# Taking the weights of a later phase in two steps, in slots shared with the input rows

## The chip, the cores and the metric

The kernel runs on one core of a Trainium2 chip. A core has five engines with queues of their own: TensorE (matrix products, PE in the profile, with its weight loads as PEld), VectorE (DVE), ScalarE (ACT), GpSimd (POOL) and SyncE (SP), which here issues all DMA transfers. Each engine works through a list of instructions that is fixed beforehand; an instruction that needs something of another engine or of a transfer waits for a semaphore, and what stands behind it on its engine waits with it. The metric is the device time of one execution in microseconds (us); lower is better.

## The reference

One decoder layer over 4096 tokens of width 1024: an RMSNorm, one input projection, two groups of heads on its output, and an output projection with residual and a last norm.

```python
h = _rmsnorm(x, norm_gain[layer])
p = h @ w_in[layer]                               # 1024 -> 4224 columns: 33 blocks of 128
ps = p[..., :SHIFT_WIDTH]                         # blocks 0 to 12
ps = ps + (_token_shift(ps) - ps) * shift_mix[layer]
...                                               # RWKV-7 recurrence on ps -> y_a
z_a = p[..., o0:o0 + c_a]                         # blocks 13 to 16
...                                               # q, k, v, z_b: blocks 17 to 32
y_b = _dilated_attention(_rope_partial(q, pos), _rope_partial(k, pos), v)
...                                               # silu gates on y_a and y_b
x = x + jnp.concatenate([y_a, y_b], axis=-1) @ w_out[layer]
return _rmsnorm(x, final_gain)
```

Weights and inputs are float32. The kernel computes large products in float16 with every operand split into two parts (the rounded value and the rest), so a weight block must first be scaled by a power of two, taken from its largest absolute value, and then split.

## The kernel before

The program has four stages in a row: the front, an RWKV phase into which the fill is woven, attention, and the output projection. The front normalises and transposes x, computes blocks 0 to 12 for all tokens, and prepares the other 20 blocks of `w_in` for the fill, which multiplies them later.

The front goes over tiles of 512 tokens, j = 0 to 7. `load_x(j)` loads four blocks of 128 rows (`xr`, four slots), squares and scales them on ScalarE, and transposes them on TensorE in eight groups of four (`xp`, line 404), each into a PSUM tile with the tag `proj`, which has two slots; ScalarE, VectorE and GpSimd make the sums and parts from it (`ss`, `xa`, `xb`, `xc`). `single(j)` multiplies block 12 (`pf`, line 529), `pair(q, j)` for q = 0 to 5 two blocks each by a seven-product scheme (`ps`, line 537). `shift` mixes neighbouring tokens into `o` (three slots) and stores it to `prs`.

Between the pairs of tiles 2 to 7 stands one task each: eight `out_max` (the largest of `w_out`), 20 `spill` and four `out_weights` (splitting `w_out`, with two loads `wor` and 14 stores `wos`). The order of tasks is a list: `tasks = [(out_max, n) for n in range(8)] + [(spill,)] * 4`, then four times `out_weights` and three spills, then four spills. `load_x(j + 1)` is written behind pair 1 of tile j.

A spill (`spill_weights`, line 314) of block b does all of this in one piece: load 512 KB into `wr` (one slot, shared with the loads of `w_out`); the largest absolute value of each row on VectorE (line 266) into `wsm`; the largest over the rows by two small matmuls into a `proj` tile (`max`, lines 274 and 276) with a VectorE reduction between; the power of two and its reciprocal; the two parts into `wl` (line 293 on ScalarE, line 294 on VectorE; one slot, lent to the second load of `out_weights` too); the store of `wl` to `wz` in DRAM (line 320).

What is written here is not the order in which the engines run. A scheduler in the framework goes through the program with its own cost estimates, gives each tile a slot when one is free, places each engine's instructions one by one, earlier written first where several are ready, and fixes that order. So an instruction can move past others when the tiles or slots around it change.

After tile 7, `first_fill` and `fill_weights` load the first operands of the fill, whose products (`pj`, line 706) begin where the front's end; the RWKV phase begins with small loads, whose tiles lie where the front's tiles lay, and its first matmul is `pu` (line 852).

Of the kernel before, what the change touches and what calls it, by code (L numbers as in the profile page):

```python
# [12 lines left out]
F32 = mybir.dt.float32  # L13
# [9 lines left out]
NKT = 8  # L23
# [10 lines left out]
WTOP = 2.0 ** 14  # L34
# [154 lines left out]
class Layer:  # L189
# [71 lines left out]

    def power(self, sm, *xs):

        V = self.nc.vector
        for i, x in enumerate(xs):
            V.tensor_reduce(sm[:, i:i + 1], x, axis=AX.XY if len(x.shape) > 2 else AX.X, op=ALU.max,
                            apply_absolute_value=True)
        if len(xs) > 1:
            V.tensor_max(sm[:, 0:1], sm[:, 0:1], sm[:, 1:2])

        ps = self.RP.tile([128, 132], F32, tag="proj", name=f"max{self.nsum}")
        self.nsum += 1
        P = self.nc.tensor
        P.matmul(ps[0:1, 0:128], lhsT=sm[:, 0:1], rhs=self.ident, start=True, stop=True)
        V.tensor_reduce(sm[0:1, 1:2], ps[0:1, 0:128], axis=AX.X, op=ALU.max)
        P.matmul(ps[:, 128:129], lhsT=self.ones[0:1, :], rhs=sm[0:1, 1:2], start=True, stop=True)
        V.tensor_scalar(sm[:, 1:2], ps[:, 128:129], 1e-30, None, op0=ALU.max)
        V.tensor_scalar(sm[:, 0:1].bitcast(I32), sm[:, 1:2].bitcast(I32), 0x7F800000, None, op0=ALU.bitwise_and)
        V.reciprocal(sm[:, 2:3], sm[:, 0:1])

    def scale(self, wr, b, top, pool):

        V, n = self.nc.vector, len(wr)
        sm = pool.tile([128, 3], F32, tag="wsm", name=f"wsm{b}", bufs=2)
        self.power(sm, *wr)
        V.tensor_scalar(self.usc[:, b:b + n], sm[:, 0:1].to_broadcast([128, n]), self.g2, 1.0 / (top * XS),
                        op0=ALU.mult, op1=ALU.mult)
        V.tensor_scalar(sm[:, 2:3], sm[:, 2:3], top, None, op0=ALU.mult)
        return sm[:, 2:3]
# [21 lines left out]
            V.tensor_scalar(self.ug[:, z:z + 1], self.usc[:, 21 + z:22 + z], self.uh[:, z:z + 1], 1.0 / QS,  # L311
                            op0=ALU.mult, op1=ALU.mult)

    def spill_weights(self, b, pool):

        wr = pool.tile([128, NKT, 128], F32, tag="wr", name=f"wr{b}", bufs=1)
        w = pool.tile([128, 2, NKT, 128], F16, tag="wl", name=f"wl{b}", bufs=1)
        self.load_weights(wr, b)
        self.parts(w, wr, self.scale([wr], b, WTOP, pool))
        self.nc.sync.dma_start(self.wz[b - 13], w)  # L320
        if b < 17:
            self.gate_scales(b - 13, b)
        elif b > 28:
            self.gate_scales(b - 25, b)
# [27 lines left out]
    def front(self):  # L352
# [5 lines left out]
        V, G, S, P = nc.vector, nc.gpsimd, nc.scalar, nc.tensor  # L358
# [3 lines left out]
        sp = ctx.enter_context(tc.tile_pool(name="sF", bufs=2))  # L362
# [71 lines left out]
        def first_fill():  # L434
            self.nx = 0
            self.fx = self.fill_load(0)

        def spill():
            if later:
                self.spill_weights(later.pop(0), sp)  # L440

        def weight_slot():

# [120 lines left out]
        later = [17, 18, 19, 20, 13, 14, 21, 22, 23, 24, 15, 16, 25, 26, 27, 28, 29, 30, 31, 32]  # L564
        pairs, free = [[] for _ in range(6)], []
        with tc.high_priority(offset=HP0):
            xa, xb, xc = load_x(0)
        wr = sp.tile([128, NKT, 128], F32, tag="wr", name="wr12", bufs=1)
# [5 lines left out]
        steps = [(pair_weights, 0), (single, 0), (load, 1), (pair, 0, 0), (pair_weights, 1), (single, 1), (pair, 0, 1),  # L574
                 (pair_weights, 2), (pair, 1, 0), (pair, 1, 1), (pair_weights, 3), (pair, 2, 0), (pair, 2, 1),
                 (pair_weights, 4), (pair_weights, 5)]
        steps += [(pair, q, 0) for q in range(3, 6)] + [(load, 2)] + [(pair, q, 1) for q in range(3, 6)]
        tasks = [(out_max, n) for n in range(8)] + [(spill,)] * 4
        for n in range(4):
            tasks += [(out_weights, n)] + [(spill,)] * 3  # L580
        tasks += [(spill,)] * 4
        for j in range(2, T // TF):
            steps.append((single, j))
            for q in range(6):
                steps.append((pair, q, j))
                if q == 1 and j + 1 < T // TF:
                    steps.append((load, j + 1))
                if tasks:
                    steps.append(tasks.pop(0))
                if j == T // TF - 1 and q == 2:  # L590
                    steps.append((first_fill,))
                if j == T // TF - 1 and q in (0, 1):
                    steps += [(self.fill_weights, 0, n) for n in (range(0, 3), range(3, 6))[q]]
        for fn, *args in steps:
            fn(*args)
        ctx.close()
        self.F = self.Rc.enter_context(tc.tile_pool(name="F", bufs=1, side="right"))

# [1045 lines left out]
```

## Time and profile before

| | us |
|---|---|
| median of 3 runs | 3585.1 |
| lowest and highest | 3569.59, 3585.86 |
| profiled execution | 3583.38 |
| its span, first to last instruction | 3581.6 |
| TensorE busy | 3161.2 (88%) |
| VectorE busy | 2213.0 (62%) |
| ScalarE busy | 1881.2 (53%) |
| GpSimd busy | 1317.5 (37%) |
| mean granted TensorE clock | 0.936 of full |

The page shows the span in slices with each engine's busy share. TensorE is at nine tenths or more in most slices of the middle, and lower at the beginning, in three places of the front, and in attention. A share over the whole program says little on a change in one stage; the front is read by stretches, by waits (which names the instruction that released each idle time) and in order of time. In a row of a timeline stand the start, the duration, engine, line, operation, result and operands, the form and the count, and in brackets the idle time before it and what ended that.

### The profile page before, as it was taken

To read this page: it belongs to the slowest core of one execution; us is meant where nothing else is said; L and a number is where in the kernel's file an instruction comes from. 1 tells how busy PE (TensorE), PEld (TensorE's weight loads), DVE (VectorE), ACT (ScalarE), POOL (GpSimd) and SP (SyncE) were. 2 spreads that over 40 slices of the span, in tenths; PEclk is the share of its full clock that TensorE was granted. 3 is DMA by queue.
4 is the path that set the end of the run, shared out by engine and by line. 5 is a ranking of instruction groups with operands and counts; after the bars stand their busy time and mean duration, and the time that the engine had idled before them with its cause. 6 is when DMAs were issued, how large, how long until landed. Compare 5 with 4: busy or idle time off the path is not lost. (4 is left out here: it accounts for less than half of the span.)

```text
span 3581.6 us, 74520 instructions
## 1 busy us (share of the span) xinstructions
PE 3161.2 (88%) x27788; PEld 2458.3 (69%) x27788; DVE 2213.0 (62%) x5525; ACT 1881.2 (53%) x4174; POOL 1317.5 (37%) x1357
## 2 busy tenths in 40 slices
PE   5989957768999999999999999978788888977878
PEld 4778846657878878788766766767677777743333
DVE  7766745546776676677766667554465555246666
ACT  6455535334555656566645555532566667843333
POOL 4432312223232333334322223200445555656655
PEclk7999979889999999999999999988799999989989
DMA  6234545645454654545533334365755556467553
GB/s 194 88 133 145 163 132 159 195 135 154 121 139 124 183 138 121 143 122 144 154 108 106 105 102 116 79 165 152 146 97 99 100 109 111 124 187 209 169 196 112
DMA packets 644875, 490.59 MB, mean 137 GB/s; under 512 B 329457, under 2 KB 570865, under 8 KB 639473
## 3 DMA queue, kind: packets, MB, share of 16 engines
q1 hardware_dynamic: 644512, 485.83, 50.8%
q8 instruction: 219, 3.59, 0.4%
q14 instruction: 144, 1.17, 0.1%
HBM read 307.65 MB, written 177.77 MB: 136 GB/s over the span
## 5 line engine op out<-in xcount | busy, mean ns | idle before, releaser
L706 PE MATMUL pj<-xF,wf 128*128 128x256 f16 x5376 | 695.7, 278 | 16.1 <-ACT qhl L717 7.5
L706 PEld LDWEIGHTS <-wf 128*128 128x128 f16 x5376 | 503.3, 99 | 113.9 <-issue 17.3
L1319 POOL TENSOR_TENSOR hl<-pt,hl 128x1024 f16<-128x1024 f32 x192 | 368.3, 1928 | 291.5 <-ACT hl L1317 253.9
L537 PEld LDWEIGHTS <-wF 128*128 128x128 f16 x4032 | 395.0, 99 | 93.1 <-issue 38.0
L1559 PE MATMUL o<-wo,yc 128*128 128x512 f16 x1344 | 320.6, 401 | 78.7 <-DVE uC L1579 54.0
L1253 DVE CUSTOM_DVE_ANT_0 jk<-sm,at 128x256 bf16<-128x256 f32 (+1 forms) x768 | 257.9, 388 | 194.4 <-PE sm L1246 192.5
L1310 ACT ACTIVATE pt<-st,pb,esc 128x512 f32<-128x512 f32 (+1 forms) x344 | 257.4, 776 | 194.1 <-PE st L1307 186.3
L1559 PEld LDWEIGHTS <-yc 128*128 128x128 f16 x1344 | 136.6, 103 | 256.8 <-issue 99.9
L1329 PE MATMUL po<-hl,vt 128*128 128x128 f16 (+1 forms) x3528 | 291.5, 234 | 11.0 <-POOL hl L1319 5.5
L537 PE MATMUL ps<-xb,wF 128*128 128x256 f16 x2304 | 279.1, 275 | 20.1 <-ACT xb L422 9.0
L1329 PEld LDWEIGHTS <-vt 128*128 128x128 f16 x3528 | 251.9, 101 | 28.6 <-issue 11.9
L1062 DVE SCALAR_TENSOR_TENSOR S<-S,WC,zy 64x64 f32<-64x64 f32 x512 | 142.7, 279 | 139.6 <-PE zy L1059 104.2
L537 PE MATMUL ps<-xa,wF 128*128 128x256 f16 x1728 | 216.0, 275 | 13.2 <-DVE u L552 11.2
L1246 PE MATMUL sm<-km,qm 66*128 66x256 f16 (+1 forms) x768 | 133.1, 277 | 79.1 <-DMA vt<-vsc 47.6
L1307 PE MATMUL st<-q,k 66*128 66x256 f16 (+1 forms) x768 | 184.9, 271 | 0.0
L1307 PE MATMUL st<-qhh,kst 128*128 128x256 f16 (+1 forms) x768 | 184.3, 270 | 0.0
L687 PE MATMUL pv<-wf,xF 128*128 128x512 f16 x768 | 183.6, 380 | 0.0
L1317 ACT CAST hl<-pt 128x1024 f16<-128x1024 f32 x192 | 181.1, 951 | 3.5 <-PE po L1329 1.0
L881 POOL TENSOR_TENSOR BK<-kk,sg 128x256 f32<-128x256 f32 x64 | 64.5, 1008 | 211.4 <-DVE sg L857 122.1
L1246 PEld LDWEIGHTS <-qm 66*128 66x128 f16 x768 | 78.0, 123 | 89.9 <-issue 34.1
L1299 PE MATMUL st<-at 128*128 128x512 bf16 (+1 forms) x352 | 136.2, 391 | 1.1 <-ACT pt L1310 1.0
L916 PE MATMUL pg<-KR,BK 64*128 64x128 f32 x1024 | 132.6, 290 | 4.6 <-DVE BK L887 2.5
(287 smaller groups left out, 6886.6 us busy)
## 6 DMA issues: line engine op xcount, KB each, us to landing
xF<-xsc SPq DMA_DIRECT2D x96, 512.0 KB
prs<-o SPq DMA_DIRECT2D x96, 256.0 KB
krv<-prs SPq DMA_DIRECT2D x64, 384.0 KB
wr<-in_w_in_dram SPq DMA_DIRECT2D x33, 512.0 KB
xr<-in_x_dram SPq DMA_DIRECT2D x32, 512.0 KB
xZ<-xsc SPq DMA_DIRECT2D x64, 256.0 KB
gC<-gsc SPq DMA_DIRECT2D x16, 1024.0 KB
xo<-in_x_dram SPq DMA_DIRECT2D x32, 512.0 KB
```

What stands on the lines that cost most here:

```text
L537: P.matmul(ps[:, 0:HT], lhsT=w[:, u, q % HK, :], rhs=x[:, v, q % HK, :], start=(start and q == 0), stop=(q == 3 * HK - 1), skip_group_chec ...
L687: P.matmul(ps, lhsT=x[v][:, k, s * 128:(s + 1) * 128], rhs=self.fw["v", 2 * u + k // 4][:, k % 4], start=(q == 0), stop=(q == 23))
L706: P.matmul(ps, lhsT=self.fw[b][:, u, k, :], rhs=x[v][:, k, :], start=(q == 0), stop=(q == 23))
L1062: V.scalar_tensor_tensor(Sbd[p][hc, hc], Sbd[p][hc, hc], WC[hc, c:c + 1], bank[hc, 2, hc], op0=ALU.mult, op1=ALU.add)
L1246: P.matmul(ps[:, n % 2, 256 - w:], lhsT=tok(qm[0:66], d, c, n * 128, 128), rhs=chunks(km[0:66], d, c, lo, w), start=True, stop=True)
L1253: V.tensor_tensor_reduce(jk[:, :w], ps[:, r % 2, 256 - w:], mask[:, i, 256 - w:256], 1.0, -3e38, op0=ALU.add, op1=ALU.max, accum_out=mx[:, ...
L1307: P.matmul(ps[:, at_:at_ + w], lhsT=tok(lh, d, c, n * 128, 128), rhs=chunks(rh, d, c, q0 * 128, w), start=False, stop=not st, skip_group_c ...
L1310: S.activation(pt[:, to:to + at_], ps[:, :at_], AF.Exp, scale=esc[:, p:p + 1], bias=pb[:, 0:1])
L1317: S.copy(hl[:, 0, :n], pt[:, :n])
L1319: (G if nsp[0] % HLG[0] < HLG[1] else V).tensor_sub(hl[:, 1, :n], pt[:, :n], hl[:, 0, :n])
L1329: P.matmul(out, lhsT=v[:, b * VW + v0:b * VW + v0 + 128], rhs=rhs, start=start and v0 + part == 0, stop=True, skip_group_check=True)
L1559: P.matmul(ps, lhsT=x[:, v, q % HK, :], rhs=w[:, u, q % HK, :], start=(start and q == 0), stop=(q == 3 * HK - 1), skip_group_check=True)
```

## The change

The spill is cut in two. `spill_start` loads the block and takes the row maxima; its `wr` now takes one of the four slots of the tag `xr`, which the rows of x use. `spill_end` does the rest: the largest over rows, the scale, the parts into `wl`, the store. `power` and `scale` are cut at the same place into `largest` and `power_of`, and `scale` and `scale_of`; other callers of them do what they did. A task `spill` now calls `spill_start` and puts the block on a list; a step `spilled` right behind it ends the oldest block on the list if two are waiting. When no block is left to start, the rest are ended at once. So block n is ended behind the start of block n + 1, a task or more later.

```diff
+    def largest(self, sm, *xs):
+        V = self.nc.vector
         for i, x in enumerate(xs):
             V.tensor_reduce(sm[:, i:i + 1], x, ...)
...
+    def power_of(self, sm):
+        V = self.nc.vector
         ps = self.RP.tile([128, 132], F32, tag="proj", name=f"max{self.nsum}")
...
+    def scale_of(self, sm, n, b, top):
+        V = self.nc.vector
+        self.power_of(sm)
...
-    def spill_weights(self, b, pool):
-        wr = pool.tile([128, NKT, 128], F32, tag="wr", name=f"wr{b}", bufs=1)
+    def spill_start(self, b, pool):
+        wr = pool.tile([128, NKT, 128], F32, tag="xr", name=f"wr{b}", bufs=4)
+        sm = pool.tile([128, 3], F32, tag="wsm", name=f"wsm{b}", bufs=2)
+        self.load_weights(wr, b)
+        self.largest(sm, wr)
+        return b, wr, sm
+
+    def spill_end(self, pool, b, wr, sm):
         w = pool.tile([128, 2, NKT, 128], F16, tag="wl", name=f"wl{b}", bufs=1)
-        self.load_weights(wr, b)
-        self.parts(w, wr, self.scale([wr], b, WTOP, pool))
+        self.parts(w, wr, self.scale_of(sm, 1, b, WTOP))
         self.nc.sync.dma_start(self.wz[b - 13], w)
...
+        spilling = []
         def spill():
             if later:
-                self.spill_weights(later.pop(0), sp)
+                spilling.append(self.spill_start(later.pop(0), sp))
+        def spilled():
+            if len(spilling) > 1 or not later:
+                self.spill_end(sp, *spilling.pop(0))
...
                 if tasks:
-                    steps.append(tasks.pop(0))
+                    task = tasks.pop(0)
+                    steps.append(task)
+                    if task[0] is spill:
+                        steps.append((spilled,))
...
         for fn, *args in steps:
             fn(*args)
+            if fn is spilled and not later:
+                while spilling:
+                    spilled()
```

The diff does not tell where the scheduler puts things; the engines' orders do. Names carry the tile or block number (`xp6_0_0` is a transpose for tile 6, rows half 0; `max16` is the max of block 22, `max17` of block 23; `ps5_4_2` is a product of pair 4 of tile 5).

TensorE at the end of tile 5 before, where the transposes of tile 6 begin:

```order
L537 MATMUL ps5_5_3_6284<-xb5_4625,wF21_1512 128x256
L274 MATMUL max16_5354<-cst_60,wsm22_5352 1x128
L276 MATMUL max16_5354<-wsm22_5352,cst_60 128x1
L274 MATMUL max17_5540<-cst_60,wsm23_5538 1x128
L404 MATMUL xp6_0_0_5681<-cst_60,xr6_0_1_5670 128x128
L404 MATMUL xp6_0_0_5681<-cst_60,xr6_0_0_5668 128x128 x2
L404 MATMUL xp6_0_0_5681<-cst_60,xr6_0_1_5670 128x128
```

and the place where the transposes of tile 6 begin now:

```order
L562 LDWEIGHTS wF17_1471
L562 MATMUL ps5_4_2_6137<-xa5_4611,wF17_1471 128x256
L422 MATMUL xp6_0_0_5668<-cst_60,xr6_0_1_5657 128x128
L422 MATMUL xp6_0_0_5668<-cst_60,xr6_0_0_5655 128x128 x2
L422 MATMUL xp6_0_0_5668<-cst_60,xr6_0_1_5657 128x128
L422 MATMUL xp6_0_1_5686<-cst_60,xr6_0_1_5657 128x128
L422 MATMUL xp6_0_1_5686<-cst_60,xr6_0_0_5655 128x128 x2
L422 MATMUL xp6_0_1_5686<-cst_60,xr6_0_1_5657 128x128
```

The first transposes of tile 6 stood behind the last product of tile 5 and two maxima; now they stand among the products of pair 4 of tile 5. max16 stands 258 matmuls ahead of them, and max17 follows after the transposes, at the beginning of tile 6. The second half (`xp6_1`) stands at the end of tile 5.

TensorE at the end of tile 7 before, with the beginning of the fill:

```order
L537 MATMUL ps7_5_3_8124<-xb7_6731,wF21_1512 128x256
L537 LDWEIGHTS wF21_1512
L537 MATMUL ps7_5_3_8124<-xb7_6731,wF21_1512 128x256
L274 MATMUL max25_7301<-cst_60,wsm29_7299 1x128
L276 MATMUL max25_7301<-wsm29_7299,cst_60 128x1
L274 MATMUL max26_7432<-cst_60,wsm30_7430 1x128
L276 MATMUL max26_7432<-wsm30_7430,cst_60 128x1
L274 MATMUL max27_7620<-cst_60,wsm31_7618 1x128
L276 MATMUL max27_7620<-wsm31_7618,cst_60 128x1
L274 MATMUL max28_7757<-cst_60,wsm32_7755 1x128
L706 LDWEIGHTS wf0_0_7634
L706 MATMUL pj0_17_8299<-xF0_0_7889,wf0_0_7634 128x256
```

and now:

```order
L562 MATMUL ps7_5_3_8124<-xb7_6718,wF21_1512 128x256
L562 LDWEIGHTS wF21_1512
L562 MATMUL ps7_5_3_8124<-xb7_6718,wF21_1512 128x256
L737 LDWEIGHTS wf0_0_7619
L737 MATMUL pj0_17_8299<-xF0_0_7889,wf0_0_7619 128x256
L737 LDWEIGHTS wf0_0_7619
L737 MATMUL pj0_17_8299<-xF0_0_7889,wf0_0_7619 128x256
```

The four maxima between the last product and the fill have moved in among the products of tile 7; the last of them, max28, now stands 172 matmuls before the end of that tile.

SP's queue where the rows of tile 5 are loaded before (`prs` are stores of `o`):

```order
L514 DMA prs_81<-o3_4_3873 128x512
L514 DMA prs_81<-o3_5_3891 128x512
L381 DMA xr5_0_0_4628<-in_x_dram 128x1024
L381 DMA xr5_0_1_4630<-in_x_dram 128x1024
L514 DMA prs_81<-o3_6_4002 128x512
L514 DMA prs_81<-o3_7_4020 128x512
L381 DMA xr5_1_0_4714<-in_x_dram 128x1024
L381 DMA xr5_1_1_4716<-in_x_dram 128x1024
```

and where the last of these four row blocks is loaded now (`wor` and `wos` are the loads and stores of `out_weights`):

```order
L511 DMA wos_115<-wov0_1_4483 128x4x128 x2
L511 DMA wos_115<-wov0_4_4488 128x4x128 x2
L511 DMA wos_115<-wov0_5_4494 128x4x128 x2
L505 DMA wor1_5181<-in_w_out_dram 128x8x128
L511 DMA wos_115<-wov1_0_5185 128x4x128
L399 DMA xr5_1_1_4703<-in_x_dram 128x1024
L253 DMA wr13_4790<-in_w_in_dram 128x8x128
L511 DMA wos_115<-wov1_0_5185 128x4x128
L539 DMA prs_81<-o4_4_4896 128x512
L539 DMA prs_81<-o4_5_4914 128x512
L539 DMA prs_81<-o4_6_5027 128x512
```

The load of `xr5_1_1` stood directly behind the others of its tile. Now the other three stand behind the stores of blocks 17, 18 and 19, one behind each, and this one behind the whole of `out_weights(0)` and the first store of `out_weights(1)`.

More of the change, by code (lines that the diff above doesn't have):

```diff
@@ L262, in power @@
     def power(self, sm, *xs):
+        self.largest(sm, *xs)
+        self.power_of(sm)
+    def largest(self, sm, *xs):
         V = self.nc.vector
@@ L281, in scale @@
     def scale(self, wr, b, top, pool):
-        V, n = self.nc.vector, len(wr)
         sm = pool.tile([128, 3], F32, tag="wsm", name=f"wsm{b}", bufs=2)
-        self.power(sm, *wr)
+        self.largest(sm, *wr)
+        return self.scale_of(sm, len(wr), b, top)
+    def scale_of(self, sm, n, b, top):
+        V = self.nc.vector
+        self.power_of(sm)
         V.tensor_scalar(self.usc[:, b:b + n], sm[:, 0:1].to_broadcast([128, n]), self.g2, 1.0 / (top * XS),
```

## The prediction

> **What bounds the kernel now.** I read the busy time by stretch first, cutting the front where the single product of each tile of 512 tokens ends. The columns are the stretch and its length, then busy time (and instructions) of TensorE matmul, weight load, VectorE, ScalarE and GpSimd, then the granted TensorE clock, the DMA share and GB/s.
>
> ```profile
> 223.00:287.00 64.00, 62.72 (x573) 56.14 (x571) 38.94 (x95) 37.03 (x78) 18.75 (x36) 1.00 0.34 122
> 287.00:355.00 68.00, 65.86 (x596) 58.13 (x595) 42.33 (x109) 38.12 (x79) 18.95 (x36) 1.00 0.36 129
> 355.00:426.00 71.00, 67.25 (x599) 58.09 (x597) 54.01 (x124) 43.41 (x86) 24.53 (x39) 1.00 0.50 157
> 426.00:552.00 126.00, 78.47 (x625) 64.11 (x624) 66.08 (x157) 50.29 (x93) 25.52 (x42) 0.78 0.47 139
> 552.00:644.00 92.00, 73.57 (x598) 60.65 (x596) 57.15 (x134) 48.38 (x93) 29.78 (x43) 0.89 0.54 156
> 644.00:701.00 57.00, 56.34 (x505) 48.62 (x502) 31.15 (x68) 17.42 (x31) 5.77 (x24) 1.00 0.69 221
> 701.00:741.00 40.00, 3.78 (x14) 1.83 (x14) 14.55 (x38) 4.26 (x5) 0.63 (x4) 0.55 0.44 116
> ```
>
> A tile without spills (223 to 287) takes 64 us, nearly all of it matmul: 573 of them, 0.11 us each. Tiles 4, 5 and 6 (from 355) have much the same matmuls and take 71, 126 and 92; tile 7, which transposes no next tile, takes 57, and after it come 40 us in which TensorE does almost nothing. Against 64 (57 for tile 7) that is 7 + 62 + 28 + 40 = 137 us of loss. No other engine is full in any row. What TensorE waits for in 355 to 755, longest in total first (us, times, longest):
>
> ```profile
> PE max L274 <- DVE wsm L266: 74.4, 13, 24.0
> PE xp L404 <- ACT ss L412: 14.1, 9, 4.6
> ```
>
> 74.4 us is the small matmul that turns a block's row maxima, waiting for the reduction. One spill in order of time, all engines:
>
> ```profile
> 504.40 0.46 SPq L253 DMA_DIRECT2D wr<-in_w_in_dram  x1
> 508.77 1.22 DVE L266 TENSOR_REDUCE wsm<-wr 128x1 f32<-128x1024 f32 x1 [4.84 <-DMA wr<-in_w_in_dram]
> ...
> 510.04 0.59 PE L274 MATMUL max<-cst,wsm 128*1 128x128 f32 x2 [24.02 <-DVE wsm L266]
> ...
> 512.39 1.15 ACT L293 ACTIVATE wl<-wr,wsm 128x1024 f16<-128x1024 f32 x1 [9.25 <-DVE wsm L288]
> 513.57 1.28 DVE L294 SCALAR_TENSOR_TENSOR wl<-wr,wsm,wl 128x1024 f16<-128x1024 f32 x1 [1.22 <-ACT wl L293]
> 514.88 0.33 SPq L320 DMA_DIRECT2D wz<-wl  x1
> ...
> 521.51 0.58 PE L274 MATMUL max<-cst,wsm 128*1 128x128 f32 x2 [9.93 <-DVE wsm L266]
> 522.03 1.11 PE L404 MATMUL xp<-cst,xr 128*128 128x128 f32 x4
> ```
>
> The block `wr` has one slot, so the next load is issued only after the parts: the load takes 4.4 us (504.40 to 508.77), reduction to parts 6.1, and the next max comes 11.5 after the last with nothing beside it. Only at 522.03 do the transposes of tile 6 start, because two maxima stand ahead of them on TensorE. The end of the front, on TensorE alone:
>
> ```profile
> 692.56 0.38 PE L274 MATMUL max<-cst,wsm 128*1 128x128 f32 x2
> ...
> 699.32 1.47 PE L537 MATMUL ps<-xb,wF 128*128 128x256 f16 x12
> 706.60 0.59 PE L274 MATMUL max<-cst,wsm 128*1 128x128 f32 x2 [5.80 <-DVE wsm L266]
> ...
> 718.24 0.59 PE L274 MATMUL max<-cst,wsm 128*1 128x128 f32 x2 [9.65 <-DVE wsm L266]
> ...
> 740.72 0.58 PE L274 MATMUL max<-cst,wsm 128*1 128x128 f32 x2 [9.55 <-DVE wsm L266]
> 741.24 4.66 PE L706 MATMUL pj<-xF,wf 128*128 128x256 f16 x21
> ...
> 760.82 0.37 PE L852 MATMUL pu<-hl,lru 128*128 128x256 f32 x1
> ```
>
> The products are done at 701, four spills are not, and the fill phase stands behind their maxima. So the serial chain of spills sets the front's length, by way of TensorE's order.
>
> **The change part by part.** No arithmetic is added or removed: 20 loads, 20 reductions, 20 pairs of small matmuls, 20 pairs of parts. What changes is when they stand.
>
> *The maxima.* Each load now has a slot of its own a task or more before its max. By the rows of TensorE's order shown with the change, max16 stands 258 matmuls ahead of the transposes of tile 6, rather than in front of them, and the last max 172 matmuls before the end of tile 7, rather than behind it. Then the wait of 74.4 goes, and the 40 us after tile 7 go to 0, if the spills keep up. What paces them next is `wl`, still one slot: parts 1.15 + 1.28, the issue, and the landing of the store, for which the last spill gives the price (SP's row, then the GpSimd row that waits for it):
>
> ```profile
> 749.75 0.34 SPq L320 DMA_DIRECT2D wz<-wl  x1
> 752.56 0.53 POOL L806 MEMSET Xst<- 128x512 f32 x1 [50.93 <-DMA wz<-wl]
> ```
>
> 2.8 us; so a spill can follow another every 5.6. In tile 7 max21 to max28 stand 357 matmuls apart, 39 us, 5.6 a step on average and 6 to 9 in the later half. It just fits. I take 0; the bounds are 0 and 15 (a third more per step).
>
> *The rows of x* now share the four `xr` slots with the spills. By the rows of SP's order, three of the four loads of tile 5 follow one spill's store each, and the last one has been moved past the whole first w_out block and the first piece of the second; queued behind it on SP are a weight load and the `o` stores, for which ScalarE's shift waits when its three `o` slots are full. Lengths, from SP's rows:
>
> ```profile
> 397.09 0.38 SPq L480 DMA_DIRECT2D wor<-in_w_out_dram  x1
> ...
> 403.08 0.38 SPq L480 DMA_DIRECT2D wor<-in_w_out_dram  x1
> 406.18 1.79 SPq L486 DMA_DIRECT2D wos<-wov  x2
> ...
> 434.21 0.46 SPq L253 DMA_DIRECT2D wr<-in_w_in_dram  x1
> ...
> 483.96 0.38 SPq L480 DMA_DIRECT2D wor<-in_w_out_dram  x1
> ```
>
> From its second load a w_out block takes 31.1 us (403.08 to 434.21), or 20.4 with idle engines (483.96 to 504.40); I take 26. From its first load to its first store are 9.1 (397.09 to 406.18). When the first spill's parts end, when TensorE comes to the first max, and what a row block costs on ScalarE:
>
> ```profile
> 336.77 0.38 PE L274 MATMUL max<-cst,sc 128*1 128x128 f32 x2
> 347.52 1.28 DVE L294 SCALAR_TENSOR_TENSOR wl<-wr,wsm,wl 128x1024 f16<-128x1024 f32 x1 [0.75 <-ACT wl L293]
> L385 ACT ACTIVATE xsq<-xr x30: 1040/1044/1057, 4.6 to 580.0; 128x1024 bf16<-128x1024 f32 x30
> L394 ACT ACTIVATE xr<-xr,xst x30: 1132/1136/1154, 8.6 to 585.5; 128x1024 f32<-128x1024 f32 x30
> ```
>
> Tile 5: first parts done at about 349 as now, third store at 361 (two more rounds of 5.6), landed at 364, which frees `wl` for the block's second load; block done 390, first piece of the next 398, row block landed 402.5 (4.4), squared and scaled about 406 (1.04 + 1.13 and the small steps between). TensorE reaches those transposes 542 matmuls behind the first max, which now stands 28 matmuls later than at 336.77: at 399. Stall 7 us, bounds 0 and 15 by the two lengths of a block. By the same steps tile 6 waits 7 (0 to 20: its second row block follows a spill whose `wl` is lent to w_out), and tile 7 waits 10 (0 to 25: 7 for max20, whose reduction stands behind such a spill's parts on VectorE, and 3 for rows).
>
> *What stays uncovered.* The second halves of tiles 6 and 7 are still transposed at the end of the tile before. All eight groups of tile 6, uncovered, ran from 522.03 to here:
>
> ```profile
> 547.19 1.91 PE L529 MATMUL pf<-xa,w 128*128 128x256 f16 x16 [0.85 <-ACT xa L420]
> ```
>
> 25.2 us. Half is 12.6, less some 30 matmuls that run in between: 9 for each of the two, bounds 3 and 13.
>
> *Sum.* A max costs TensorE 0.8 (two rows of 0.38). Tile 4: 64 + 1 + 7 = 72. Tile 5: 64 + 4 + 7 + 9 = 84. Tile 6: 64 + 3 + 10 + 9 = 86. Tile 7: 57 + 2 = 59. Gap: 0. That is 301 against 71 + 126 + 92 + 57 + 40 = 386, so 85 less. The RWKV phase's first matmul came 19.6 us after the fill's (741.24 to 760.82) behind 104 fill matmuls, 11.4 us; now 122 stand ahead, 13.4 us, and its loads wait for the last `o` store instead of the last spill. I take 18.5 and 2 us of fill done ahead, 3 gained, bounds -4 and 6. In all 88 less.
>
> The Trainium skill (TensorE: Matmul & The Clock Gate, section "HAM oscillation — how this bites in real kernels") says that an idle gap above some 3.4 us halves the array's clock, until it has been busy about as long again. The clock column above agrees: 0.78, 0.89 and 0.55 in the stretches with gaps. By that rule each of my three waits would cost 1.7 us more, an estimate, and the sum would be 83.
>
> *What comes after* shifts whole, since TensorE is nearly full there too:
>
> ```profile
> 1100.00:1200.00 100.00, 100.00 (x963) 82.89 (x962) 69.68 (x155) 60.98 (x179) 32.45 (x38) 1.00 0.54 147
> ```
>
> The profiled execution took 3583.4 us, 1.8 of it outside its span of 3581.6 and 1.7 below the median of 3585.1. 3583.4 - 88 = 3495.
>
> **Rivals.**
> *The rows of x come too late, and it is slower.* Place: SP, behind w_out. If a block takes its 31 us (5 more), the transposes come wholly uncovered (25.2 rather than 9, 16 more), and the `o` stores queued behind the late row hold the products for another 13, then three tiles lose 34 each, 102 in all: 14 slower than before, 3597. It decides from 29 us a tile (88 / 3). For it: SP's order. Against: TensorE's order covers at least half of each tile's transposes, and nothing of that was in the tiles before.
> *The spills still set the pace.* At the tail's 11.5 us a spill (706.60 to 718.24 and the next), the eight of tile 7 take 92 rather than 59, 33 lost: 55 less than before, 3528. For it: one `wl` slot, and ScalarE's and VectorE's waits for it hold all behind them. Against: the load, 4.4 of the 11.5, is now ahead.
> *Everything is covered.* The waits (24) and the uncovered halves (18) go too: 130 less, 3453. For it: in 223 to 287 a whole tile is transposed without loss. Against: the order leaves four groups at the end of tiles 5 and 6.
> *Nothing is gained*, if the fill did not wait for the spills alone: 3583. Against it, in the gap nothing else is busy (VectorE 14.55 of 40).
>
> **How the numbers follow.** My forecast has 0.62; the spills' pace (3510 to 3550) 0.18; all covered (3450 to 3470) 0.12; late rows, slower, 0.05; nothing gained 0.03. The range 3460 to 3538 leaves out the last two, half of the covered case and a little of the pace. A measurement of this kernel tells some 0.5%, 18 us, from no change: faster 0.91, same 0.04, slower 0.05.
>
> **What would show it.** Right: the wait of the max matmul falls from 74.4 to below 20; the fill starts right behind tile 7, near 656; tiles 4 to 7 take 72, 84, 86, 59; TensorE waits about 24 us for row blocks and one max. Wrong: a gap stays after tile 7, or a tile passes 100 us with TensorE waiting for transposes.

## The result, and the profile after

The changed kernel takes 3489.0 us in the median of four runs (3485.9 to 3494.4), the kernel before beside it 3583.7. The ratio is 0.9745, with a 95% interval of 0.9717 to 0.9774: faster by some 81 to 101 us. The profiled execution took 3487.4 us, its span is 3485.7.

The front by stretches, cut as in the prediction where the single product of each tile ends. The columns are the same as there. First come tile 2 and tile 3, then 4, 5, 6 and 7; the last row is the beginning of the fill.

```profile
220.00:284.00 64.00, 62.73 (x572) 56.14 (x571) 38.92 (x95) 37.02 (x78) 18.70 (x36) 1.00 0.34 127
284.00:351.00 67.00, 67.00 (x604) 58.77 (x603) 42.99 (x115) 38.83 (x81) 18.40 (x36) 1.00 0.36 121
351.00:421.00 70.00, 67.10 (x602) 58.43 (x600) 48.48 (x132) 44.47 (x89) 24.19 (x40) 1.00 0.65 191
421.00:512.00 91.00, 79.89 (x633) 65.04 (x631) 60.42 (x149) 46.78 (x91) 24.02 (x40) 0.91 0.62 186
512.00:597.00 85.00, 73.12 (x598) 60.63 (x595) 67.35 (x144) 50.52 (x96) 32.15 (x44) 0.92 0.67 195
597.00:651.00 54.00, 54.00 (x477) 45.73 (x476) 35.66 (x92) 18.33 (x29) 4.44 (x21) 1.00 0.72 260
651.00:700.00 49.00, 46.84 (x423) 40.68 (x421) 25.05 (x48) 22.68 (x59) 16.74 (x24) 1.00 0.58 162
```

The row with 40 us of nearly nothing is gone: behind tile 7 comes the fill, at full clock. Tiles 5 and 6 still lose time, and in both the clock is below 1. All that TensorE waited for in the max matmuls and in the transposes from 340 to 670 (engine, what waits, what released it; us, times, longest):

```profile
PE max L282 <- ACT ss L430: 5.2, 2, 3.6
PE max L284 <- DVE wsm L283: 1.5, 2, 1.1
PE xp L422 <- ACT ss L430: 0.2, 1, 0.2
PE xp L422 <- ACT xr L412: 0.2, 1, 0.2
```

Line 282 is the old line 274 and 271 the old 266 (row maxima). The 74.4 us of the max matmul behind the row maxima have no row any more. The end of the front, on TensorE:

```profile
649.86 1.47 PE L562 MATMUL ps<-xa,wF 128*128 128x256 f16 x12
651.17 0.27 PE L737 MATMUL pj<-xF,wf 128*128 128x256 f16 x1
651.27 1.47 PE L562 MATMUL ps<-xa,wF 128*128 128x256 f16 x12
652.59 1.47 PE L562 MATMUL ps<-xb,wF 128*128 128x256 f16 x12
...
668.84 0.36 PE L883 MATMUL pu<-hl,lru 128*128 128x256 f32 x1
```

The fill's first matmul comes at 651.17, before at 741.24: 90.1 us earlier. It stands ahead of the last 24 products of the front, which end at 654.06 (652.59 and 1.47), so 87 us is the fairer figure for the front. The RWKV phase's first matmul comes at 668.84 instead of 760.82, 92.0 earlier. The span is 95.9 shorter; the other 4 us lie behind that point, and are less than the 8.5 by which two profiles of the changed kernel differ there (2816.9 and 2825.4 us from the RWKV phase's first matmul to the end; before 2820.8).

### The profile page after: what moved, and what is told of

It is laid out like the page before. It is cut to its first block, busy times and chain, and to the rows that moved or that the text cites. A ratio compares the mean times of both kernels' runs of the same rounds, so it can differ in the third digit from the quotient of the medians.

```text
span 3485.7 us, 74535 instructions
## 1 busy us (share of the span) xinstructions
PE 3169.3 (91%) x27788; PEld 2461.5 (71%) x27788; DVE 2205.0 (63%) x5525; ACT 1874.9 (54%) x4174; POOL 1314.9 (38%) x1357
## 5 line engine op out<-in xcount | busy, mean ns | idle before, releaser
L737 PE MATMUL pj<-xF,wf 128*128 128x256 f16 x5376 | 688.6, 277 | 13.4 <-ACT qhl L748 11.3
L1360 PEld LDWEIGHTS <-vt 128*128 128x128 f16 x3528 | 251.7, 101 | 26.9 <-issue 11.1
L1081 ACT COPY UV<-V 64x128 f32<-64x128 f32 x256 | 75.3, 295 | 127.9 <-PE zy L1090 125.3
L865 POOL TENSOR_TENSOR l_sq<-sq,h_sq 128x256 fp32r<-128x256 f32 x64 | 54.4, 850 | 219.3 <-ACT h_sq L864 212.3
```

The lines of the kernel that those rows point to most:

```text
L737: P.matmul(ps, lhsT=self.fw[b][:, u, k, :], rhs=x[v][:, k, :], start=(q == 0), stop=(q == 23))
L1360: P.matmul(out, lhsT=v[:, b * VW + v0:b * VW + v0 + 128], rhs=rhs, start=start and v0 + part == 0, stop=True, skip_group_check=True)
```

## The experiments

Every kernel is compared with the kernel before on the same chip, by the ratio. "Fill at" is the start of the fill's first matmul in the profiled execution, which tells the front's length without what comes later. In all kernels but the first, the last 24 products run behind that mark and end 3 to 5 us after it, so the column compares them well with each other, and flatters them by as much beside the kernel before.

| kernel | median, us | ratio (95% interval) | tiles 4, 5, 6, us | fill at, us |
|---|---|---|---|---|
| before | 3584 | 1 | 71, 126, 92 | 741.2 |
| the change | 3489.0 | 0.9745 (0.9717 to 0.9774) | 70, 91, 85 | 651.2 |
| one step, shared slots | 3485.8 | 0.9713 (0.9681 to 0.9744) | 74, 77, 84 | 641.7 |
| before, no max on TensorE | 3496.3 | 0.9754 (0.9729 to 0.9779) | 75, 73, 73 | 640.8 |
| before, two `wr`, three `xr` | 3506.4 | 0.9769 (0.9745 to 0.9793) | 72, 93, 79 | 663.6 |
| the change, spills first | 3515.6 | 0.9805 (0.9780 to 0.9830) | 67, 70, 71 | 623.9 |
| the change, five slots | 3492.3 | 0.9728 (0.9708 to 0.9749) | 71, 86, 89 | 647.4 |
| the change, two `wl` | 3480.2 | 0.9700 (0.9674 to 0.9726) | 71, 77, 81 | 629.2 |
| the same, one step | 3477.0 | 0.9676 (0.9653 to 0.9699) | 74, 73, 80 | 627.5 |
| the change, two `wl`, w_out spread | 3478.1 | 0.9687 (0.9668 to 0.9707) | 70, 78, 77 | 623.4 |
| the change, rows earlier | 3481.4 | 0.9705 (0.9676 to 0.9735) | 71, 70, 86 | 637.2 |
| the change again | 3497.7 | 0.9751 (0.9725 to 0.9777) | 70, 91, 87 | 655.3 |
| all three edits | 3463.2 | 0.9653 (0.9626 to 0.9680) | 70, 74, 74 | 621.5 |

### Is it the slots or the two steps?

The step that ends a block no longer leaves one block waiting:

```diff
         def spilled():
-            if len(spilling) > 1 or not later:
+            if spilling:
                 self.spill_end(sp, *spilling.pop(0))
```

> The changed kernel without its two steps: a block's end is written right behind its own start, as before the change, but the block still lies in one of the four slots of the input rows. Theory A (the loads ahead are what helps: in the kernel before, one slot ties the next load to the last parts, and the max of a spill is placed on TensorE before its block has come; with four slots the block is there): nearly all of the gain stays, 3489 to 3500 us, and the wait of the max matmul for the reduction stays below 20 us in the front. Rival B (the two steps are what helps, since the end is written a task later than the start and so the max stands further back on TensorE): most of the gain goes, 3550 to 3585 us, and the max matmul waits 50 us or more.

3485.8 us, ratio 0.9713, and of the max matmul's waits in the front these are all that end on VectorE:

```profile
PE max L284 <- DVE wsm L283: 2.0, 3, 1.2
PE max L284 <- DVE wsm L286: 1.2, 1, 1.2
PE max L282 <- DVE wsm L285: 0.9, 1, 0.9
```

Theory A. The two steps give nothing; without them the ratio is, if anything, lower. The same pair with two slots of parts (below) goes the same way: 0.9700 with the two steps, 0.9676 without. Each pair's intervals overlap, so a loss by the two steps is not shown in the time; in the front the first pair differs by 9.5 us (641.7 against 651.2), the second by 1.7.

Then the other way round: the kernel before in one piece, with a second slot for the block, and a row slot less to make room:

```diff
-        wr = pool.tile([128, NKT, 128], F32, tag="wr", name=f"wr{b}", bufs=1)
+        wr = pool.tile([128, NKT, 128], F32, tag="wr", name=f"wr{b}", bufs=2)
...
-                    xr.append(sp.tile([128, D], F32, tag="xr", name=f"xr{j}_{i}_{h}", bufs=4))
+                    xr.append(sp.tile([128, D], F32, tag="xr", name=f"xr{j}_{i}_{h}", bufs=3))
```

> The kernel before, spill in one piece, but with two slots for the weight blocks instead of one, and three slots for the rows of x instead of four, so that it takes no more room and nothing is shared. Theory A (it is enough that the next block can be loaded while the last one is worked on; sharing the row slots and the two steps do nothing by themselves): 60 to 95 us go, 3490 to 3525 us, with the fewer row slots costing some of it. Rival B (a block must be two or three tasks ahead, which only the four shared slots give): less than 40 us go, 3545 to 3585, and the max matmul still waits 40 us or more for the reduction.

Ratio 0.9769, so 83 us of some 91, and the wait of 74.4 us is this:

```profile
PE max L274 <- DVE wsm L266: 8.5, 7, 1.7
```

Theory A again: one block ahead is nearly enough, even with one row slot less.

### Is the loss the chain of spills, or what stands behind its max?

In the kernel before, the spill's scale becomes a constant; the two small matmuls and the reduction between them go:

```diff
-        self.parts(w, wr, self.scale([wr], b, WTOP, pool))
+        V.tensor_reduce(sm[:, 1:2], wr, axis=AX.XY, op=ALU.max, apply_absolute_value=True)
+        V.tensor_scalar(sm[:, 0:1], sm[:, 1:2], 0.0, 0.125, op0=ALU.mult, op1=ALU.add)
...
+        self.parts(w, wr, sm[:, 2:3])
```

> The kernel before, with one slot and one step, in which a spill no longer takes the largest value over the rows: the two small matmuls and the reduction between them are left out and a constant takes the place of the scale, while load, row maxima, reciprocal, parts and store stay. Theory A (the loss of the kernel before is TensorE standing behind a max whose block has not come; the transposes and the fill stand behind it too): TensorE has nothing of a spill in its list, so 80 to 100 us go, 3485 to 3505 us, although the spills still follow each other serially. Rival B (the serial chain of spills through one slot sets the length of the front, whoever waits for it): the chain is only some 2 us shorter for each of the 20 spills, so 0 to 40 us go, 3545 to 3585 us.

Ratio 0.9754, the gain of the whole change. The chain is still there, and nearly as slow. SP's rows of the last spills, each a store and the next load:

```profile
635.84 0.32 SPq L327 DMA_DIRECT2D wz<-wl  x1
636.25 0.39 SPq L253 DMA_DIRECT2D wr<-in_w_in_dram  x1
646.49 0.32 SPq L327 DMA_DIRECT2D wz<-wl  x1
646.86 0.43 SPq L253 DMA_DIRECT2D wr<-in_w_in_dram  x1
657.00 0.34 SPq L327 DMA_DIRECT2D wz<-wl  x1
```

One spill each 10.5 to 10.7 us, against 11.5 in the tail before, and the last one ends after the fill has begun. TensorE no longer stands in it:

```profile
644.50 1.47 PE L544 MATMUL ps<-xb,wF 128*128 128x256 f16 x12
645.82 4.53 PE L713 MATMUL pj<-xF,wf 128*128 128x256 f16 x40
660.58 7.09 PE L713 MATMUL pj<-xF,wf 128*128 128x256 f16 x45 [10.23 <-ACT qhl L724]
```

So the chain through one slot cost what it did only because a matmul of each spill stood in TensorE's list ahead of work that was ready. What remains of it is a single wait of 10.2 us for ScalarE, which ends 3.6 us behind the last store of parts. (For this kernel "fill at" tells too little: the fill starts 10 us earlier than in the change, but with this wait the RWKV phase starts at 667.62, in the change at 668.84.)

### What makes tiles 5 and 6 slow?

The prediction gave them 84 and 86 us: rows of x loaded late because of w_out, and transposes uncovered for it. The first test takes w_out away from there:

```diff
-        tasks = [(out_max, n) for n in range(8)] + [(spill,)] * 4
-        for n in range(4):
-            tasks += [(out_weights, n)] + [(spill,)] * 3
-        tasks += [(spill,)] * 4
+        tasks = [(out_max, n) for n in range(8)] + [(spill,)] * 20
+        tasks += [(out_weights, n) for n in range(4)]
```

> The changed kernel with its list of tasks put in another order: all 20 spills come before the four blocks of w_out, which then fall on the last four tasks, in tiles 6 and 7. Theory A (the prediction's: in tiles 5 and 6 the rows of x come late or uncovered because w_out's loads and stores stand ahead of them on the transfer queue): tiles 5 and 6, 91 and 85 us in the changed kernel, fall to 70 to 75, tile 7 grows by the blocks of w_out to 60 to 75, and the time falls by 5 to 25 us to 3464 to 3484. Rival B (what is lost in tiles 5 and 6 is the work of the tasks on VectorE and ScalarE, which is the same in any order): the loss moves to the tiles with the tasks and the time stays at 3480 to 3495. Rival C (four blocks of w_out at the end do not fit in tile 7): a gap between tile 7 and the fill of 15 to 40 us, and 3500 to 3530.

Tiles 5 and 6 fall to 70 and 71, as theory A has it, and the fill starts 27 us earlier than in the change. But the total is some 21 us worse by the ratios: rival C decides it, with another place and size than it gave. The gap is not between tile 7 and the fill, but 9 us behind the fill's first matmul (623.86):

```profile
627.91 5.29 PE L735 MATMUL pj<-xF,wf 128*128 128x256 f16 x47
682.02 7.19 PE L735 MATMUL pj<-xF,wf 128*128 128x256 f16 x48 [48.82 <-ACT qhl L746]
689.32 0.36 PE L881 MATMUL pu<-hl,lru 128*128 128x256 f32 x1
```

ScalarE, which must empty the fill's PSUM tiles, was still splitting w_out; two of its waits from 615 to 700:

```profile
ACT wov L305 <- DMA wor<-in_w_out_dram: 17.5, 3, 8.2
ACT wov L305 <- DMA wos<-wov: 13.9, 7, 2.9
```

So w_out is better placed inside the front, where TensorE has other work.

The second test moves the rows alone, one task earlier:

```diff
-                if q == 1 and j + 1 < T // TF:
+                if q == 0 and j + 1 < T // TF:
                     steps.append((load, j + 1))
```

> The changed kernel with the rows of the next tile written behind pair 0 of a tile instead of behind pair 1, so that they take their slots one task earlier, and nothing else changed. Theory A (tile 5 takes 91 us because its row blocks are loaded late: ScalarE waits for them, VectorE stands behind ScalarE, TensorE behind VectorE, and the array's clock drops): tiles 5 and 6 together, 176 us, lose 8 to 20, and so does the time, ratio 0.968 to 0.973. Rival B (the tasks' own work and stores on ScalarE and VectorE make the loss, whenever the rows come): tiles 5 and 6 together stay within 6 us, ratio 0.973 to 0.977.

Tiles 5 and 6 together take 156 us against 178 in the change on the same chip, ratio 0.9705 against 0.9751 (the intervals still touch): theory A. Nearly all of it, 20.8 us, is in tile 5; tile 3 grows by 2. The rows of tiles 5 and 6:

```profile
426.10:496.40 70.30, 67.22 (x601) 58.37 (x599) 53.27 (x134) 45.63 (x89) 25.24 (x40) 1.00 0.67 201
496.40:582.40 86.00, 72.72 (x626) 61.61 (x624) 65.24 (x149) 49.64 (x95) 31.15 (x45) 0.96 0.66 191
```

VectorE still has 53 us of work in the 70 of tile 5. That is 7 less than in the change, but tiles 3, 4 and 7 have more, and from tile 3 to 7 it works 253 us where it worked 255. So the tasks' work is there as before; what is gone from tile 5 is the idle time and the slow clock. Tile 6 keeps its 86 us with the rows earlier, so late rows are not shown to be its cause. What shortens it is w_out placed elsewhere (71 us with the spills first) and, by less, the second `wl` (81, below). The change itself, run once more beside it, came to ratio 0.9751 (first 0.9745) and tile 5 to 91.1, as expected:

> The changed kernel as it is, once more, to stand on the same chip beside the next two. If the spread between programs is as in the runs so far: a ratio to the kernel before of 0.972 to 0.977, and in the profile the fill's first matmul at 648 to 655 us with tile 5 at 86 to 95 us.

### One slot of parts, and the number of shared slots

Two kernels put the other weight loads (`wr12`, `out_max`, `out_weights`, and pair 5's) into the shared slots too. One spends the room on a fifth slot, the other on a second `wl`:

The slots of the first, then of the second:

```diff
-        wr = pool.tile([128, NKT, 128], F32, tag="xr", name=f"wr{b}", bufs=4)
+        wr = pool.tile([128, NKT, 128], F32, tag="xr", name=f"wr{b}", bufs=5)
```

```diff
-        w = pool.tile([128, 2, NKT, 128], F16, tag="wl", name=f"wl{b}", bufs=1)
+        w = pool.tile([128, 2, NKT, 128], F16, tag="wl", name=f"wl{b}", bufs=2)
```

> The changed kernel with five slots shared by the rows, the spills and all other weight loads, instead of four for rows and spills and one for the others: the same room. Theory A (rows of x that come late for want of a slot cost tile 5 and 6 some 10 us each, by way of ScalarE, which waits for them, and VectorE behind it): rows are loaded a slot earlier, tiles 5 and 6 take 70 to 82 instead of 91 and 85, and 5 to 20 us go, 3469 to 3484. Rival B (rows are late because of what stands ahead of them on the transfer queue, and of the one slot of parts): no change, 3484 to 3495.

> The changed kernel with two slots for a spill's parts instead of one; the room comes from the single slot of the other weight loads, which now share the four slots of the input rows too. Theory A (the one slot of parts is the next pace: ScalarE waits 14 us in tiles 5 and 6 for the store of the last parts, and what stands behind it on ScalarE and VectorE makes TensorE wait): 5 to 20 us go, 3469 to 3484, and ScalarE's wait for the store goes to below 5. Rival B (those waits are off the path that sets the end, and the four slots are now shared by still more loads): no change or a few us more, 3485 to 3500, with TensorE waiting for rows of x.

Five slots: 0.9728, tiles 5 and 6 at 86 and 89: rival B. The two `wl`: 0.9700, tiles at 77 and 81, the fill 22 us earlier than in the change. ScalarE's wait for the store of the last parts, with five slots from 340 to 600 and then with two `wl` from 344 to 632:

```profile
ACT wl L305 <- DMA wz<-wl: 13.8, 5, 3.9
```

```profile
ACT wl L305 <- DMA wz<-wl: 1.5, 1, 1.5
```

So it is the slot of parts that counts there, not the number of shared slots. The second load of a w_out block borrows a `wl` slot too, and which of the two uses counts was not separated. In the total the interval of two `wl` still touches that of the change; in the front the difference is plain. The row blocks' loads stand behind these stores on SP, so this and the late rows are partly one cause.

### A faster version

> The changed kernel with both edits that gained so far: a block is ended right behind its start, and the parts have two slots, with the other weight loads in the four shared slots. If the two steps do nothing: the same as two slots of parts alone, 3472 to 3486. If the two steps keep a block in its slot a task longer and so hold the rows of x back: 5 to 10 us less than that, 3465 to 3476.

> The changed kernel with two slots of parts and another order of tasks: the four blocks of w_out come one to a tile, third in tiles 3 to 6 behind the rows of the next tile in the program, each followed by five spills; before they came at 1 and 5 of tile 4, 3 of tile 5 and 1 of tile 6. Theory A (two blocks of w_out at the side of one tile's rows make tile 5 slow, and one each does not): no tile over 80 us, 3460 to 3475, and the start of the RWKV phase stays 17 to 18 us behind the fill's. Rival B (a block of w_out costs a tile some 8 to 10 us wherever it stands): the same sum over tiles 3 to 6, 3475 to 3490.

The first came to a median of 3477.0, as if the two steps did nothing, and to a ratio of 0.9676, some 3468 us beside a kernel before of 3584, as if they cost a little: it does not decide. The second keeps the two `wl` and moves w_out's blocks to one a tile:

```diff
+        tasks = [(out_max, n) for n in range(8)]
+        for n in range(4):
+            tasks += [(out_weights, n)] + [(spill,)] * 5
```

0.9687, no tile over 78, and the RWKV phase starts 17.5 us behind the fill, as theory A has it. But beside the two `wl` alone (0.9700, fill at 629.2) the fill starts only 6 us earlier, tiles 3 to 6 take 290 us together instead of 295, and the ratios' intervals overlap: spreading by itself changed little, which is nearer to rival B. Beside the change the fill starts 28 us earlier, the profiled span is only 8 shorter, and the median is some 21 us better by the ratios. Two things lie between: on its chip the kernel before takes 3591.2 us, 7 more than where the change was measured, and what follows the RWKV phase's first matmul scatters, from 2817 to 2837 us over the thirteen profiles. An earlier fill does not by itself lose its lead there: with two `wl` alone that rest takes 2819.6.

> The changed kernel with the three edits that shortened the front: one step instead of two, two slots of parts with the other weight loads in the shared slots, and one block of w_out to a tile. If they add up in the front: the fill's first matmul at 612 to 622 us instead of 651, ratio 0.962 to 0.967. If the front has no more to give (its tiles 4 to 6 are near 70 us each already): as one block of w_out to a tile alone, 622 to 627 and 0.967 to 0.970.

3463.2 us, ratio 0.9653 (0.9626 to 0.9680), beside 0.9751 (0.9725 to 0.9777) for the change on the same chip: a better kernel than the change and the one before. The front (621.5) lies just inside what was expected if the three add up, 612 to 622, but only 2 us below that with two `wl` and w_out spread (623.4), and the intervals of the two ratios overlap. That the single step adds to these two is not shown.

## Why the prediction was right

The predicted time was 3495 us, the measured one 3489.0, inside the range of 3460 to 3538. By its steps:

**What bounds the kernel.** Right. The loss was TensorE standing behind maxima whose blocks had not come: taking the max out of TensorE's list, with the chain left as it was, gives the whole gain, and so do slots without two steps. What the prediction did not say is that the two steps of the change are not needed for it.

**The sum.** Predicted 72 + 84 + 86 + 59 + 0 = 301, measured 70 + 91 + 85 + 54 + 0 = 300; the gain in these rows 86 against 85. Counted with the 24 products behind the mark, tile 7 takes 57 and the gain is 83. From the fill's first matmul to the RWKV phase's pass 17.7 us instead of 19.6, 1.9 gained where 3 were put down; without those products the gain there is 4.8. The front was already 4 us ahead at the end of tile 3 (351 against 355), which had no term. So part of the agreement is luck: tile 5 was 7 too low, tile 7 by these cuts 5 too high, and those cancel.

**The rows of x** are the step that was mis-sized. For tile 5's rows, used in tile 4, a stall of 7 was taken. It was at most 2.9, the whole idle time of tile 4 (70.00 less 67.10), and none of that is booked to rows: the w_out block took 21.5 us, not the 26 chosen between 20.4 and 31.1, and the row block behind it was issued at 390.86, not about 398. Tile 4 came near its 72 all the same because it holds 602 matmuls, 67.1 us, rather than the 573 of the tile that the sum starts from.

```profile
363.92 0.38 SPq L505 DMA_DIRECT2D wor<-in_w_out_dram  x1
...
385.42 0.46 SPq L505 DMA_DIRECT2D wor<-in_w_out_dram  x1
390.41 0.36 SPq L511 DMA_DIRECT2D wos<-wov  x1
390.86 0.46 SPq L399 DMA_DIRECT2D xr<-in_x_dram  x1
```

For tile 6's rows, used in tile 5, 7 for the stall and 9 for the uncovered half were taken, and by the test with earlier rows they cost 20 to 21. "TensorE waits about 24 us for row blocks and one max" did not show: its waits for rows are 0.2. The lateness can reach it by a detour. In order of time, SP, ScalarE, VectorE and TensorE in tile 5:

```profile
475.55 0.34 SPq L399 DMA_DIRECT2D xr<-in_x_dram  x1
...
479.36 1.06 ACT L403 ACTIVATE xsq<-xr 128x1024 bf16<-128x1024 f32 x1 [1.96 <-DMA xr<-in_x_dram]
480.54 0.17 DVE L407 TENSOR_SCALAR xst<-xst 128x2 f32<-128x2 f32 x1 [1.03 <-ACT xsq L403]
...
481.02 1.22 DVE L271 TENSOR_REDUCE wsm<-wr 128x1 f32<-128x1024 f32 x1
...
482.69 2.97 DVE L536 SCALAR_TENSOR_TENSOR o<-c,sc,o 128x512 f32<-128x512 f32 x3
...
485.92 0.41 DVE L579 TENSOR_TENSOR c<-u,ps 128x256 f32<-128x256 f32 x1
486.38 2.40 PE L562 MATMUL ps<-xb,wF 128*128 128x256 f16 x12 [4.78 <-DVE c L579]
```

ScalarE waits for the row block, VectorE for the square, and then a reduction, three `o` and four small operations stand ahead of the `c` that empties TensorE's PSUM tile. The wait is booked to VectorE, 4.8 us, though a row block is what came late. Of the 4.8, ScalarE's 1.96 us are the late row; how much of the rest follows from it this row does not show. That the 20 us of the tile go when the rows are loaded earlier is shown only in sum, by the run with earlier rows. Tile 5 splits as follows: at tile 4's 0.1115 us a matmul (67.10 / 602) its 633 take 70.6; the idle time is 91.0 - 79.9 = 11.1; 9.3 are left. A mean clock of 0.91 over 91 us accounts for at most 8.2 of them; the last 1 fits 12 more rows of max matmuls than in tile 4, at 0.19 us each instead of 0.11.

**The clock.** The main sum left it out and gave it a sentence beside: 83 less instead of 88. In tiles 5 and 6 it cost at most 8.2 and, by the same steps, some 6.5 (73.12 less 598 at 0.1115), so up to 15 rather than the 5 of that sentence. By the rule named there (the Trainium skill, TensorE: Matmul & The Clock Gate, section "HAM oscillation — how this bites in real kernels") gaps above some 3.4 us count; the trace here shows the clock fall behind shorter ones too (last section).

**The spills' pace.** The term of 0 held for the tail: the last store of parts is issued at 639.98, 11 us before the fill.

```profile
634.12 0.32 SPq L338 DMA_DIRECT2D wz<-wl  x1
...
639.98 0.32 SPq L338 DMA_DIRECT2D wz<-wl  x1
```

The 5.86 us between the two are close to the 5.6 that were worked out. In tiles 5 and 6 the one slot did cost something, by holding ScalarE and SP: with a second one, which w_out's loads can use too, these tiles take 18 less. The rival had the place wrong (the tail), not the cause: one slot of parts.

**Uncovered halves.** They were there, at the end of tile 5:

```profile
488.57 1.82 PE L422 MATMUL xp<-cst,xr 128*128 128x128 f32 x8
...
502.49 3.57 PE L554 MATMUL pf<-xa,w 128*128 128x256 f16 x16 [0.21 <-ACT xa L438]
```

13.9 us, with 30 products in between; less these, at 0.11 us, it is 10.6, and the term, worked out the same way, was 9. With the rows a task earlier tile 5 has 3.1 us of idle time in all (70.30 - 67.22), so this was mostly a result of the late rows.

**Tile 6.** 85 for 86, but only in part by its terms. The second half of the next tile's transposes is at its end, as predicted. The 10 us for late rows and a late max were 3.9 at the max matmuls (3.6 of it for ScalarE, not for the row maxima) and nothing booked to rows, and with the rows earlier the tile still takes 86. TensorE waits another 7.7 us for VectorE at the products, and the clock takes some 6.5. What makes VectorE late in tile 6 stays open; with the spills first, that is with w_out moved away, the tile takes 71.

**Tile 7.** 54, not 59: 477 matmuls lie between the cuts, 505 before, 28 fewer, and no gap. 24 of them are the last products, at 651.27 and 652.59, which run behind the fill's first matmul. With these the tile takes 57.

**The rivals.** "Nothing is gained" and "slower" are out. "The rows come too late" named a real cause and was far off in price: 20 us in one tile, not 34 in each of three. "Everything is covered" (3453) is close to what the version with all three edits reaches, 3463.

## What to carry to other kernels

A small instruction on the critical engine that waits for a transfer costs all that stands behind it in that engine's list; here a second buffer for what it waits for was worth 83 us, the shared slots 91, and splitting the task in two steps nothing. Price a late transfer by what it holds in every list, not at the first consumer: look who else stands behind the engine that waits, and expect the wait to be booked to another name. Work that is moved away from a crowded stage is moved to another one: w_out put last made the front 27 us shorter and the kernel some 21 us longer than the change.

## What the runs showed of the hardware

The granted clock falls after gaps of quite different length. In the changed kernel a gap of 1.75 us in front of 468.58 was followed by matmuls at about half speed (22 in 3.99 us), and one of 1.99 us in front of 399.36 by none (12 in 1.47 us, full speed). TensorE's rows, and then the clock (third column from the end) by stretch:

```profile
399.36 1.47 PE L562 MATMUL ps<-xa,wF 128*128 128x256 f16 x12 [1.99 <-ACT u L573]
...
468.58 0.27 PE L562 MATMUL ps<-xa,wF 128*128 128x256 f16 x1 [1.75 <-DVE u L577]
...
470.18 3.99 PE L562 MATMUL ps<-xa,wF 128*128 128x256 f16 x22
```

```profile
394.59:398.01 3.42, 2.77 (x26) 2.34 (x24) 2.62 (x9) 3.08 (x7) 0.04 (x1) 1.00 0.57 156
398.01:401.42 3.41, 2.02 (x17) 1.66 (x17) 3.34 (x9) 2.94 (x5) 3.20 (x3) 1.00 0.40 154
...
466.27:469.69 3.42, 1.50 (x13) 1.03 (x11) 1.50 (x3) 3.42 (x4) 0.00 (x0) 1.00 0.67 193
469.69:473.10 3.41, 3.41 (x18) 2.55 (x17) 2.52 (x11) 3.41 (x11) 0.00 (x0) 0.50 0.00 0
```

So the length of a gap does not tell here whether the clock falls. The stretches above are cells of a grid of 3.41 us, on which every stretch of halved clock in this trace begins (50 of them). The gap of 1.99 us falls on two cells, in which TensorE is busy for 2.77 and 2.02 us, and the clock stays. The gap of 1.75 us lies within one, with 1.50 us of work, and the next cell has half the clock although TensorE is busy throughout. Over the trace, a cell at full clock that is busy for less than 45% was followed by a halved one in 37 of 45 cases, and one busy for more than 55% in 10 of 857. That is a reading of one trace, not a rule tested by a run; by it, where a short wait falls counts as much as its length. Here the wait of 1.75 us cost 1.5 us more: at 0.1115 us the 22 matmuls would take 2.5 us, not 3.99.
